# Expert stage of a hybrid encoder block: ScalarE and VectorE in an order written by steps, and two rows in one split

## The chip, the cores and the metric

The kernel runs on one core of a Trainium2 chip. A core has five engines with queues of their own: PE (TensorE, matrix products; PEld in the profile is its weight load), ACT (ScalarE), DVE (VectorE), POOL (GpSimd) and SP (SyncE, which here issues transfers). Each works its instructions off in order; semaphores hold an instruction until what it needs is there. The metric is the device time of one launch in microseconds (us), lower is better.

## The reference

The reference computes one encoder block on x, 1024 tokens of width 2048: attention over a 2D neighbourhood and a two-sided long convolution side by side, an output projection, and a mixture of 16 experts. Only the experts matter here:

```python
affinity = softmax(h @ w_router)              # 1024 x 16
gate, idx = top_k(affinity.T, 128)            # every expert picks its 128 best tokens
xg = h[idx]                                   # 16 x 128 x 2048
a  = xg @ w_gate                              # 2048 -> 1024, per expert
up = xg @ w_up
ye = (silu(a) * up) @ w_down                  # 1024 -> 2048
out[idx] += ye * gate
```

All of it is float32. Each expert has 24 MB of weights, which are read once.

## The kernel before

A float32 product is made of three products in fp32r: an operand is split into hi (a cast to fp32r) and lo (the operand minus hi), and hi x hi, lo x hi and hi x lo are added up in PSUM. `split` (lines 58 to 61) does this with two instructions: ScalarE casts (L60), VectorE subtracts (L61). `mm` (L68) is one matmul.

The block runs in phases: projections, attention and convolution first, then the output projection with the router, then the choice of tokens (`topk`), then the expert stage, in `phase3`. That stage starts at about 2200 us of the span and is the only one that the change touches.

**Tokens.** `gather` fetches an expert's 128 rows by an indirect DMA on POOL into xg (one buffer). `turned` transposes four blocks of 128 x 128 on TensorE (L1202) and splits the result: for xg into xh and xl (16 blocks of k), for the product of gate-up into the two planes of h3 (tile el).

**Weights.** 24 tiles of 1 MB an expert (128 x 2048, tile w) come through a ring of 18 buffers; a load goes out when the buffer's last reader is done. The first 16 hold two rows k of w_gate or w_up (alternating, columns 0 to 1023 of row 2kk, then of row 2kk + 1), the last 8 one row of w_down.

**Steps.** TensorE works in steps of six matmuls of 512 columns on one pair of split tiles wh and wl (128 x 1024, four buffers each, so ScalarE can be four steps ahead). An expert has 32 steps of gate-up (L1141 on) and 16 of down (L1168 on). In the first 24 steps of gate-up a step is one row k of one matrix, all 1024 columns, into two of four PSUM banks. The last four rows come in another order so that half of the columns is finished early: first columns 0 to 511 of all four rows, gate and up, then columns 512 to 1023. Before the change, one such step is one row k, 512 columns of gate beside 512 of up; its wh is written by two casts of 512 columns out of two tiles w, and its wl by two subtractions. After the fourth of these eight steps, `act(0)` takes Silu of the gate sums on ScalarE (L1135) and multiplies with the up sums on VectorE (L1136); after the eighth, `act(1)` does the other half. `turn(0)` and `turn(1)` transpose the products into h3. `down` ends with four copies of PSUM sums, scaled by the gate, into el (L1179), and an indirect DMA on POOL (L1180) that adds the rows to the output. During down, the next expert's xg is transposed.

**Order.** Only TensorE's instructions stand in the order of the program; for ScalarE, VectorE and POOL, a scheduler decides where they stand (L1190):

```python
with tc.manual_schedule(engines={mybir.EngineType.PE}):
```

Of the kernel before, what the change touches and what calls it, by code (L numbers as in the profile page):

```python
# [8 lines left out]
R = mybir.dt.float32r  # L9
I32 = mybir.dt.int32  # L10
U32 = mybir.dt.uint32
AF = mybir.ActivationFunctionType
# [5 lines left out]
P = 128  # L18
D = 2048
S = 1024  # L20
KD = D // P
# [3 lines left out]
NE = 16  # L25
FF = 1024
# [11 lines left out]
class Block:  # L38
# [1029 lines left out]
    def phase3(self, ctx):  # L1068
        tc, nc, a = self.tc, self.nc, self.a
        self.topk()  # L1070
        pa = ctx.enter_context(tc.tile_pool(name="pa", bufs=1, space=PSUM, reuse_waits="tile"))
        pt_ = ctx.enter_context(tc.tile_pool(name="pt3", bufs=2, space=PSUM, reuse_waits="tile"))

        ex = ctx.enter_context(tc.tile_pool(name="ex", bufs=1, reuse_waits="tile"))
        self.ring(ctx, "ewb", 2, side="right")
        self.ring(ctx, "ewc", 8)
        el = self.el = ctx.enter_context(tc.tile_pool(name="el", bufs=1, reuse_waits="tile"))
        self.ring(ctx, "ewd", 5)
        xh = el.tile([P, KD, P], R, name="xh", bufs=1)
        xl = el.tile([P, KD, P], R, name="xl", bufs=1)  # L1080

        def bank():
            return pa.tile([P, 512], F32, name="pa", bufs=6)

        def gather(e):
            if e == NE:
                return
            xg = ex.tile([P, D + 16], F32, name="xg", bufs=1)
            nc.gpsimd.indirect_dma_start(out=xg, out_offset=None, in_=self.xg[:, :],
                                         in_offset=bass.IndirectOffsetOnAxis(ap=self.idx[:, e:e + 1], axis=0))  # L1090
            return xg

        def load():
            ahead = self.EW + max(min(self.used, KD - self.EX) + self.EX, self.used)
            while self.loaded < min(ahead, NE * self.NW):
                self.load_expert()

        def raw():
            load()
            self.used += 1  # L1100
            return self.eraw.pop(0)

        def parts():
            return (el.tile([P, FF], R, name="wh3", bufs=4), el.tile([P, FF], R, name="wl3", bufs=4))

        def products(out, hi, lo, wh, wl, start, stop):

            parts_ = [(o, slice(i * 512, i * 512 + 512)) for i, o in enumerate(out)]
            for o, sl in parts_:
                self.mm(o, hi, wh[:, sl], start, False)  # L1110
                self.mm(o, lo, wh[:, sl], False, False)
            for o, sl in parts_:
                self.mm(o, hi, wl[:, sl], False, stop)

        def half(w, i):
            wh, wl = parts()
            self.split(wh, wl, w[:, i * FF:i * FF + FF])
            return wh, wl

        def gate_up(e):  # L1120


            xg = self.xg3
            rs = ex.tile([P, 16], F32, name="rs", bufs=1)
            nc.scalar.copy(rs[:, 0:1], xg[:, D:D + 1])
            ps = {}
            for n in range(2):
                for j in range(2):
                    ps[j, n] = bank()
            y = el.tile([P, 2 * FF], F32, name="el0", bufs=1)  # L1130
            h3 = el.tile([P, 2, FF // P, P], R, name="el1", bufs=1)

            def act(n):
                s = y[:, n * 512:n * 512 + 512]
                nc.scalar.activation(s, ps[0, n], AF.Silu, scale=rs[:, 0:1])  # L1135
                nc.vector.scalar_tensor_tensor(s, ps[1, n], rs[:, 0:1], s, op0=ALU.mult, op1=ALU.mult)  # L1136

            def turn(n):
                self.turned(pt_, h3[:, 0], h3[:, 1], y, n)

            for kk in range(KD // 2 - 2):  # L1141
                if kk == 2:
                    self.xg3 = gather(e + 1)
                for j in range(2):
                    w = raw() if kk or e else None
                    for i in range(2):
                        wh, wl = half(w, i) if w is not None else ready.pop(0)
                        k = 2 * kk + i
                        products([ps[j, 0], ps[j, 1]], xh[:, k], xl[:, k], wh, wl, k == 0, False)

            w = [raw() for j in range(4)]
            for n in range(2):
                for i in range(4):
                    wh, wl = parts()
                    for j in range(2):
                        sl = slice(j * 512, j * 512 + 512)
                        c = i % 2 * FF + n * 512
                        self.split(wh[:, sl], wl[:, sl], w[i // 2 * 2 + j][:, c:c + 512])
                    if n == 1 and i == 2:
                        turn(0)  # L1160
                    k = KD - 4 + i
                    products([ps[0, n], ps[1, n]], xh[:, k], xl[:, k], wh, wl, False, i == 3)
                act(n)
            return h3, y, lambda: turn(1)

        def down(e, h):
            h3, y, rest = h
            ps = [bank() for n in range(4)]  # L1168
            for k in range(FF // P):
                w = raw()  # L1170
                for c in range(2):
                    wh, wl = half(w, c)
                    products(ps[2 * c:2 * c + 2], h3[:, 0, k], h3[:, 1, k], wh, wl, k == 0, k == FF // P - 1)
                if k == 1:
                    rest()
                elif 3 <= k < 7 and self.xg3 is not None:
                    self.turned(pt_, xh, xl, self.xg3, k - 3, 2)
            for n in range(4):
                nc.scalar.activation(y[:, n * 512:n * 512 + 512], ps[n], AF.Copy, scale=self.gate[:, e:e + 1])  # L1179
            nc.gpsimd.indirect_dma_start(out=a["out"],  # L1180
                                         out_offset=bass.IndirectOffsetOnAxis(ap=self.idx[:, e:e + 1], axis=0),
                                         in_=y, in_offset=None, compute_op=ALU.add)

        self.xg3 = gather(0)
        ready = []
        with tc.issue_after(self.first_cast.ins), tc.issue_after(self.first_sub.ins):
            for j in range(2):
                w = raw()
                ready += [half(w, i) for i in range(2)]
        with tc.manual_schedule(engines={mybir.EngineType.PE}):  # L1190
            for kg in range(4):
                self.turned(pt_ if kg < 2 else pa, xh, xl, self.xg3, kg, 2)
            for e in range(NE):
                down(e, gate_up(e))
# [96 lines left out]
```

## Time and profile before

| | us |
|---|---|
| median of 3 runs | 3332.66 |
| the runs | 3318.23, 3332.66, 3337.95 |
| profiled execution, its own time | 3327.52 |
| its span in the profile | 3325.7 |
| PE busy | 3210.5 (97%) |
| DVE busy | 2331.7 (70%) |
| ACT busy | 1844.1 (55%) |

The profile shows one execution. A timeline row has the start in us from the span's beginning, the length, engine, line and operation, the tiles (out<-in), and how many alike it merges; in brackets stands how long the engine had been idle before it, and whose event ended that. Lengths of matmuls are modelled and overlap; how fast TensorE goes is read from the distance of starts.

### The profile page before, as it was taken

The numbers are of one execution on the slowest core, as the hardware profiler recorded it, in microseconds if no ns is written. First come the engines' busy times: TensorE is split into PE (matmuls) and PEld (weight loads), VectorE is DVE, ScalarE is ACT, GpSimd is POOL, SyncE is SP. The second block draws the span as 40 slices with busy tenths as digits, with TensorE's granted clock in tenths as the row PEclk, the third lists the DMA queues.
The fourth block names the chain that finished last, engine by engine and source line by source line (L and its number), as shares of the span: only waits on it lengthen the run. The fifth ranks groups of instructions, "written<-read, shape, count | busy, mean of one in ns | idle before, by whom it ended". The sixth has DMA issues, their size and how long they took to land.

```text
span 3325.7 us, 47509 instructions
## 1 busy us (share of the span) xinstructions
PE 3210.5 (97%) x17232; PEld 2794.1 (84%) x17232; DVE 2331.7 (70%) x3624; ACT 1844.1 (55%) x2957; POOL 77.3 (2%) x200
## 2 busy tenths in 40 slices
PE   8999999999999999999999999949999999999998
PEld 8899999987888888889977787748888888887886
DVE  5676776764566666667654333289999999898997
ACT  5455655543333333334454232348888888888886
POOL 0000000000000000000000000000000000000000
PEclk9999999999999999999999999979999999999999
DMA  7645555556566556665556464289999999999993
GB/s 248 200 164 163 164 179 186 173 160 209 192 198 197 190 185 196 190 202 167 178 202 230 152 231 152 102 351 360 403 390 403 403 397 394 379 394 399 395 398 116
DMA packets 286571, 830.71 MB, mean 250 GB/s; under 512 B 26340, under 2 KB 105359, under 8 KB 229760
## 3 DMA queue, kind: packets, MB, share of 16 engines
q1 hardware_dynamic: 280544, 791.12, 65.4%
q0 software_dynamic: 5648, 36.49, 4.3%
q8 instruction: 136, 2.23, 0.3%
q14 instruction: 99, 0.81, 0.1%
q10 hardware_dynamic: 144, 0.07, 0.0%
HBM read 751.71 MB, written 75.60 MB: 249 GB/s over the span
## 4 chain that ended last, share of the span: by engine, by line
PE 86%; DMA 7%; issue 2%; ACT 2%; DVE 2%; SPq 0%; POOLq 0%; POOL 0%; ACTq 0%; DVEq 0%
PE pj L68 30%; PE pa L68 29%; PE o L68 7%; PE c L68 5%; PE f L68 4%; PE a L68 3%; PE ct L79 2%; DMA w<-in_w_out_dram 2%; PE tp L1202 1%; ACT wh L60 1%; PE a L79 1%; PE ft L79 1%; DVE wl L61 1%; PE l L68 1%; DMA x<-in_x_dram 1%
## 5 line engine op out<-in xcount | busy, mean ns | idle before, releaser
L60 ACT CAST wh<-w 128x1024 fp32r<-128x1024 f32 (+3 forms) x1368 | 1067.1, 795 | 685.5 <-PE pj L68 374.2
L61 DVE TENSOR_TENSOR wl<-w,wh 128x1024 fp32r<-128x1024 f32 (+3 forms) x1368 | 1210.6, 904 | 336.2 <-ACT wh L60 280.7
L68 PE MATMUL pa<-wh,xh 128*128 128x512 f32 x1024 | 401.5, 392 | 8.4 <-ACT wh L60 8.4
L68 PE MATMUL pa<-wh,xl 128*128 128x512 f32 x1024 | 398.9, 390 | 0.0
L68 PE MATMUL o<-wh,m 128*128 128x512 f32 x1008 | 332.7, 402 | 1.8 <-ACT wh L60 1.7
L68 PE MATMUL pj<-wh,hh 128*128 128x384 f32 x896 | 315.3, 352 | 2.9 <-ACT wh L60 2.9
L68 PE MATMUL pa<-wl,xh 128*128 128x512 f32 x1024 | 317.6, 390 | 0.0
L68 PE MATMUL pj<-hh,wh 128*128 128x512 f32 x768 | 315.2, 411 | 0.0
L68 PE MATMUL pj<-hl,wh 128*128 128x512 f32 x768 | 304.9, 397 | 4.9 <-DMA hl<-lo_d 4.8
L68 PE MATMUL pj<-wl,hh 128*128 128x384 f32 x896 | 304.5, 340 | 0.0
L68 PE MATMUL pj<-wh,hl 128*128 128x384 f32 x896 | 304.1, 339 | 0.0
L68 PE MATMUL pj<-hh,wl 128*128 128x512 f32 x768 | 303.0, 395 | 0.0
L68 PE MATMUL pa<-wh,el 128*128 128x512 f32 x1024 | 281.9, 397 | 0.0
L68 PEld LDWEIGHTS pa<-wh,xh 128*128 128x128 f32 x1024 | 192.4, 188 | 51.3 <-ACT wh L60 12.7
L68 PEld LDWEIGHTS pa<-wl,xh 128*128 128x128 f32 x1024 | 192.2, 188 | 43.7 <-DVE wl L61 3.7
L68 PEld LDWEIGHTS o<-wh,m 128*128 128x128 f32 x1008 | 192.7, 192 | 41.8 <-ACT wh L60 3.4
L68 PEld LDWEIGHTS pa<-wh,xl 128*128 128x128 f32 x1024 | 192.4, 188 | 39.1
L68 PEld LDWEIGHTS pa<-wh,el 128*128 128x128 f32 x1024 | 187.3, 189 | 35.3
L68 PE MATMUL o<-wl,m 128*128 128x512 f32 x504 | 201.0, 400 | 0.3 <-DVE wl L61 0.3
L68 PEld LDWEIGHTS pj<-wh,hh 128*128 128x128 f32 x896 | 169.5, 189 | 8.7 <-ACT wh L60 3.2
L68 PEld LDWEIGHTS pj<-hh,wl 128*128 128x128 f32 x768 | 144.7, 188 | 34.7
L68 PEld LDWEIGHTS pj<-wl,hh 128*128 128x128 f32 x896 | 169.6, 189 | 2.6 <-DVE wl L61 1.1
(307 smaller groups left out, 5275.5 us busy)
## 6 DMA issues: line engine op xcount, KB each, us to landing
hl<-lo_d SPq DMA_DIRECT2D x608, 256.0 KB, 3.0
w<-in_w_down_dram SPq DMA_DIRECT2D x128, 1024.0 KB, 11.4
w<-in_w_up_dram SPq DMA_DIRECT2D x127, 1024.0 KB, 9.1
w<-in_w_gate_dram SPq DMA_DIRECT2D x127, 1024.0 KB, 9.1
w<-in_w_at_dram SPq DMA_DIRECT2D x120, 384.0 KB, 3.4
w<-in_w_out_dram SPq DMA_DIRECT2D x64, 512.0 KB, 4.2
w<-in_w_hy_dram SPq DMA_DIRECT2D x96, 256.0 KB, 3.5
Hd<-H SPq DMA_DIRECT2D x32, 513.0 KB, 4.2
```

What stands on the lines that cost most here:

```text
L60: nc.scalar.copy(hi, src)
L61: nc.vector.tensor_tensor(lo, src, hi.bitcast(F32), op=ALU.subtract)
L68: self.nc.tensor.matmul(out, w, x, start=start, stop=stop)
L79: self.nc.tensor.transpose(pt[:, i * P:(i + 1) * P], b, self.ident)
L1202: self.nc.tensor.transpose(pt[:, i * P:(i + 1) * P], src[:, c:c + (P - 1) * step + 1:step], self.ident)
```

## The change

The casts, subtractions, Silu and copies of the expert stage now stand on ScalarE and VectorE in the order in which the program is written, as TensorE's do: `manual_schedule` lists all three engines. The program is written in steps: `pieces` yields the parts of w that the steps need, in TensorE's order, `prepare` splits the next one, and each call of `products` ends with a `prepare`, so a split is always four steps ahead of its use. What has to stand between the matmuls of a step and the next split (`act`, and `out`, the scaled copies of two down sums) is handed in as `then`. `out(0)` now stands after the last step of sums 0 and 1, one step ahead of `out(1)`.

In the last eight steps of gate-up, a step is now one tile w: two rows k of one matrix, 512 columns. Its split reads both rows through a view of 2 x 512 in one cast and one subtraction, and its six matmuls go into one PSUM bank.

```diff
-        def half(w, i):
-            wh, wl = parts()
-            self.split(wh, wl, w[:, i * FF:i * FF + FF])
-            return wh, wl
+        def pieces():
+            for e in range(NE):
+                for i in range(KD - 4):
+                    w = raw()
+                    yield w[:, :FF]
+                    yield w[:, FF:]
+                w = [raw() for i in range(4)]
+                for n in range(2):
+                    for i in range(4):
+                        yield w[i].rearrange("p (i f) -> p i f", i=2)[:, :, n * 512:n * 512 + 512]
+                for k in range(FF // P):
+                    w = raw()
+                    yield w[:, :FF]
+                    yield w[:, FF:]
+
+        todo, ready = pieces(), []
+
+        def prepare():
+            w = next(todo, None)
+            if w is not None:
+                wh, wl = el.tile([P, FF], R, name="wh3", bufs=4), el.tile([P, FF], R, name="wl3", bufs=4)
+                if len(w.shape) == 3:
+                    self.split(*(x.rearrange("p (i f) -> p i f", i=2) for x in (wh, wl)), w)
+                else:
+                    self.split(wh, wl, w)
+                ready.append((wh, wl))
+
+        def products(parts, then=None):
+            wh, wl = ready.pop(0)
+            for m, (o, hi, lo, start, stop) in enumerate(parts):
+                self.mm(o, hi, wh[:, m * 512:m * 512 + 512], start, False)
+                self.mm(o, lo, wh[:, m * 512:m * 512 + 512], False, False)
+            for m, (o, hi, lo, start, stop) in enumerate(parts):
+                self.mm(o, hi, wl[:, m * 512:m * 512 + 512], False, stop)
+            if then is not None:
+                then()
+            prepare()
...
-            w = [raw() for j in range(4)]
             for n in range(2):
                 for i in range(4):
-                    wh, wl = parts()
-                    for j in range(2):
-                        sl = slice(j * 512, j * 512 + 512)
-                        c = i % 2 * FF + n * 512
-                        self.split(wh[:, sl], wl[:, sl], w[i // 2 * 2 + j][:, c:c + 512])
                     if n == 1 and i == 2:
                         turn(0)
-                    k = KD - 4 + i
-                    products([ps[0, n], ps[1, n]], xh[:, k], xl[:, k], wh, wl, False, i == 3)
-                act(n)
+                    kk, j = KD // 2 - 2 + i // 2, i % 2
+                    products([(ps[j, n], xh[:, k], xl[:, k], False, k == KD - 1) for k in (2 * kk, 2 * kk + 1)],
+                             (lambda: act(n)) if i == 3 else None)
...
+            def out(c):
+                for n in (2 * c, 2 * c + 1):
+                    nc.scalar.activation(y[:, n * 512:n * 512 + 512], ps[n], AF.Copy, scale=self.gate[:, e:e + 1])
+
             for k in range(FF // P):
...
-            for n in range(4):
-                nc.scalar.activation(y[:, n * 512:n * 512 + 512], ps[n], AF.Copy, scale=self.gate[:, e:e + 1])
...
-        with tc.manual_schedule(engines={mybir.EngineType.PE}):
+        with tc.manual_schedule(engines={mybir.EngineType.PE, mybir.EngineType.Activation, mybir.EngineType.DVE}):
```

Three places show what moves. The first is ScalarE in the last eight steps of the seventh expert's gate-up. A number behind wh names the buffer of one step, one behind w the tile that is read. Before (steps 1 to 6; 26209 is step 1, 26271 step 6):

```order
L60 CAST wh_26209<-w_25784 128x512
L60 CAST wh_26221<-w_25784 128x512
L60 CAST wh_26209<-w_25813 128x512
L60 CAST wh_26221<-w_25813 128x512
L60 CAST wh_26233<-w_25842 128x512
L60 CAST wh_26245<-w_25842 128x512
L60 CAST wh_26259<-w_25784 128x512
L60 CAST wh_26259<-w_25813 128x512
L60 CAST wh_26271<-w_25784 128x512
L60 CAST wh_26271<-w_25813 128x512
L60 CAST wh_26233<-w_25871 128x512
L60 CAST wh_26245<-w_25871 128x512
```

With the change (steps 1 to 7, then `act(0)`, then step 8):

```order
L60 CAST wh_26095<-w_25663 128x1024
L60 CAST wh_26105<-w_25692 128x1024
L60 CAST wh_26115<-w_25714 128x1024
L60 CAST wh_26125<-w_25743 128x1024
L60 CAST wh_26135<-w_25663 128x1024
L60 CAST wh_26145<-w_25692 128x1024
L60 CAST wh_26155<-w_25714 128x1024
L1159 ACTIVATE el_25857<-pa,rs 128x512
L60 CAST wh_26167<-w_25743 128x1024
```

Before, the second halves of steps 3 and 4 (26233, 26245) stand behind both halves of steps 5 and 6; now each step has one cast, in step order. Experts 7 to 16 are ordered alike before; in experts 1 to 6 the halves stand in step order:

```order
L60 CAST wh_25600<-w_25175 128x512
L60 CAST wh_25600<-w_25204 128x512
L60 CAST wh_25612<-w_25175 128x512
L60 CAST wh_25612<-w_25204 128x512
L60 CAST wh_25624<-w_25233 128x512
L60 CAST wh_25624<-w_25262 128x512
L60 CAST wh_25636<-w_25233 128x512
L60 CAST wh_25636<-w_25262 128x512
```

These are steps 1 to 4 of the sixth expert; in the change's listing the same steps have one row each, as above.

The second place is VectorE at the end of the seventh expert's gate-up, from the subtraction ahead of `act(0)`'s product to the low half of h3 (el<-tp). Before:

```order
L61 TENSOR_TENSOR wl_26303<-w_25842,wh_26302 128x512
L1136 SCALAR_TENSOR_TENSOR el_25933<-pa,rs,el_25933 128x512
L61 TENSOR_TENSOR wl_26303<-w_25871,wh_26302 128x512
L61 TENSOR_TENSOR wl_26323<-w_25900,wh_26322 128x1024
L61 TENSOR_TENSOR wl_26333<-w_25900,wh_26332 128x1024
L61 TENSOR_TENSOR el_25934<-tp_26289,el_25934 128x512
```

With the change:

```order
L61 TENSOR_TENSOR wl_26156<-w_25714,wh_26155 128x1024
L1160 SCALAR_TENSOR_TENSOR el_25857<-pa,rs,el_25857 128x512
L61 TENSOR_TENSOR wl_26168<-w_25743,wh_26167 128x1024
L61 TENSOR_TENSOR wl_26180<-w_25772,wh_26179 128x1024
L61 TENSOR_TENSOR wl_26190<-w_25772,wh_26189 128x1024
L61 TENSOR_TENSOR el_25858<-tp_26193,el_25858 128x512
```

The product now stands a half subtraction earlier, and three whole subtractions lie between it and the low half of h3, where two and a half did.

The third place is ScalarE at the end of the seventh expert's down. Before:

```order
L60 CAST xh<-tp_26502 128x512
L60 CAST wh_26568<-w_26113 128x1024
L1179 ACTIVATE el_25933<-pa,gate 128x512 x4
L60 CAST wh_26578<-w_26113 128x1024
L60 CAST wh_26590<-w_26135 128x1024
```

With the change:

```order
L60 CAST xh<-tp_26410 128x512
L1186 ACTIVATE el_25857<-pa,gate 128x512 x2
L60 CAST wh_26427<-w_25999 128x1024
L1186 ACTIVATE el_25857<-pa,gate 128x512 x2
L60 CAST wh_26439<-w_25999 128x1024
L1149 COPY rs<-xg 128x1
L60 CAST wh_26460<-w_26021 128x1024
```

Two of the four copies of down sums moved ahead of a cast, and the small copy into rs, which stood in the middle of down before, moved behind all of them. Through it, POOL's gather of the expert after next now stands behind the scatter of this one; it stood ahead of it.

## Rows read from the trace of the kernel before

**Rows 1.** The page, part 1: busy us, share of the span, instructions.

```profile
PE 3210.5 (97%) x17232; PEld 2794.1 (84%) x17232; DVE 2331.7 (70%) x3624; ACT 1844.1 (55%) x2957; POOL 77.3 (2%) x200
```

**Rows 2.** Stretches: length, busy us by engine, granted clock, DMA share, GB/s.

```profile
2285.00:2355.00 70.00, 70.00 (x321) 58.17 (x321) 64.76 (x67) 58.43 (x71) 3.07 (x2) 1.00 1.01 395
...
2705.00:2775.00 70.00, 69.16 (x315) 56.93 (x314) 63.39 (x65) 57.12 (x70) 3.09 (x2) 1.00 1.01 393
```

**Rows 3.** Timeline of POOL, experts two to four: gathers and a scatter.

```profile
2344.47 1.50 POOL L1089 DMA_INDIRECT xg<-xg,idx  x1 [62.82 <-ACT xh L60]
2348.33 1.57 POOL L1180 DMA_INDIRECT out_dram<-el,idx  x1 [2.35 <-ACT el L1179]
...
2481.03 1.53 POOL L1089 DMA_INDIRECT xg<-xg,idx  x1 [62.63 <-ACT xh L60]
```

**Rows 4.** All waits of PE, 2208 to 3326: us in total, times, longest.

```profile
PE pa L68 <- ACT wh L60: 8.4, 10, 0.8
PE tp L1202 <- DVE el L1136: 0.9, 1, 0.9
```

**Rows 5.** Timeline of PE around the seventh expert's wait.

```profile
2655.04 0.39 PE L68 MATMUL pa<-wh,xl 128*128 128x512 f32 x1
2656.27 0.50 PE L68 MATMUL pa<-wh,xh 128*128 128x512 f32 x1 [0.84 <-ACT wh L60]
2656.60 0.39 PE L68 MATMUL pa<-wh,xl 128*128 128x512 f32 x1
```

**Rows 6.** Timeline of PE: the last of the ten waits.

```profile
3283.07 0.50 PE L68 MATMUL pa<-wh,xh 128*128 128x512 f32 x1 [0.84 <-ACT wh L60]
```

**Rows 7.** Timeline of ACT, seventh expert, casts of the last eight steps.

```profile
2647.76 0.62 ACT L60 CAST wh<-w 128x512 fp32r<-128x512 f32 x1 [0.30 <-PE pa L68]
2649.12 2.19 ACT L60 CAST wh<-w 128x512 fp32r<-128x512 f32 x4 [0.74 <-PE pa L68]
...
2654.56 2.18 ACT L60 CAST wh<-w 128x512 fp32r<-128x512 f32 x4 [0.22 <-PE pa L68]
```

**Rows 8.** Groups by form from 2080 on: busy us, mean ns | idle before.

```profile
L61 DVE TENSOR_TENSOR wl<-w,wh 128x1024 fp32r<-128x1024 f32 x647 | 777.6, 1224 | 87.8 <-ACT wh L60 43.0
L60 ACT CAST wh<-w 128x1024 fp32r<-128x1024 f32 x647 | 674.7, 1055 | 160.2 <-PE pa L68 147.6 <-DMA w<-in_w_out_dram 8.1 <-PE o L68 0.3
...
L61 DVE TENSOR_TENSOR wl<-w,wh 128x512 fp32r<-128x512 f32 x248 | 160.2, 688 | 18.7 <-ACT wh L60 13.5
...
L60 ACT CAST wh<-w 128x512 fp32r<-128x512 f32 x248 | 142.1, 618 | 42.8 <-PE pa L68 30.8 <-DVE wl L61 12.0
...
L1136 DVE SCALAR_TENSOR_TENSOR el<-pa,rs,el 128x512 f32<-128x512 f32 x32 | 23.9, 745 | 1.2 <-ACT el L1135 1.2
```

**Rows 9.** Groups by form, whole span: reads that are not plain.

```profile
L244 ACT COPY raw<-pj 128x512 f32<-128x512 f32 x32 | 18.8, 586 | 35.8 <-PE pj L68 35.6
...
L668 DVE TENSOR_TENSOR Z<-Z,c 128x512 f32<-128x512 f32 x16 | 11.0, 688 | 17.2 <-PE c L68 17.2
```

**Rows 10.** Timeline of PE, output projection: one bank, three matmuls between starts.

```profile
2150.12 0.61 PE L68 MATMUL o<-wh,m 128*128 128x512 f32 x2
2150.57 0.39 PE L68 MATMUL o<-wl,m 128*128 128x512 f32 x1
2150.80 0.61 PE L68 MATMUL o<-wh,m 128*128 128x512 f32 x2
```

**Rows 11.** Timelines of DVE and PE where the sixth expert's down starts.

```profile
2593.97 0.69 DVE L61 TENSOR_TENSOR el<-tp,el 128x512 fp32r<-128x512 f32 x1
...
2595.18 1.07 PE L68 MATMUL pa<-wh,el 128*128 128x512 f32 x4
```

**Rows 12.** Timeline of ACT: the last expert's copies of down sums.

```profile
3312.46 2.62 ACT L1179 ACTIVATE el<-pa,gate 128x512 f32<-128x512 f32 x4 [3.25 <-PE pa L68]
```

**Rows 13.** DMA issues in 2285:2354, then 2490:2558: count, KB, us to landing.

```profile
w<-in_w_down_dram SPq DMA_DIRECT2D x8, 1024.0 KB, 11.9
...
w<-in_w_down_dram SPq DMA_DIRECT2D x8, 1024.0 KB, 11.4
```

More of the change, by code (lines that the diff above doesn't have):

```diff
@@ L1101, in raw @@
             return self.eraw.pop(0)
[L1103 to L1113, printed above, removed]
-        def half(w, i):
-            wh, wl = parts()
-            self.split(wh, wl, w[:, i * FF:i * FF + FF])
-            return wh, wl
+        def pieces():
[32 more added lines that the diff above has]
+            prepare()
         def gate_up(e):
@@ L1144, in gate_up @@
                 for j in range(2):
[L1145 to L1149, printed above, removed]
-            w = [raw() for j in range(4)]
+                    for k in (2 * kk, 2 * kk + 1):
+                        products([(ps[j, n], xh[:, k], xl[:, k], k == 0, False) for n in range(2)])
             for n in range(2):
                 for i in range(4):
-                    wh, wl = parts()
-                    for j in range(2):
-                        sl = slice(j * 512, j * 512 + 512)
-                        c = i % 2 * FF + n * 512
-                        self.split(wh[:, sl], wl[:, sl], w[i // 2 * 2 + j][:, c:c + 512])
                     if n == 1 and i == 2:
                         turn(0)
-                    k = KD - 4 + i
-                    products([ps[0, n], ps[1, n]], xh[:, k], xl[:, k], wh, wl, False, i == 3)
-                act(n)
+                    kk, j = KD // 2 - 2 + i // 2, i % 2
+                    products([(ps[j, n], xh[:, k], xl[:, k], False, k == KD - 1) for k in (2 * kk, 2 * kk + 1)],
+                             (lambda: act(n)) if i == 3 else None)
             return h3, y, lambda: turn(1)
@@ L1168, in down @@
             ps = [bank() for n in range(4)]
+            def out(c):
+                for n in (2 * c, 2 * c + 1):
+                    nc.scalar.activation(y[:, n * 512:n * 512 + 512], ps[n], AF.Copy, scale=self.gate[:, e:e + 1])
             for k in range(FF // P):
-                w = raw()
                 for c in range(2):
-                    wh, wl = half(w, c)
-                    products(ps[2 * c:2 * c + 2], h3[:, 0, k], h3[:, 1, k], wh, wl, k == 0, k == FF // P - 1)
+                    products([(ps[2 * c + n], h3[:, 0, k], h3[:, 1, k], k == 0, k == FF // P - 1) for n in range(2)],
+                             (lambda: out(c)) if k == FF // P - 1 else None)
                 if k == 1:
@@ L1184, in phase3 @@
         self.xg3 = gather(0)
-        ready = []
         with tc.issue_after(self.first_cast.ins), tc.issue_after(self.first_sub.ins):
-            for j in range(2):
-                w = raw()
-                ready += [half(w, i) for i in range(2)]
-        with tc.manual_schedule(engines={mybir.EngineType.PE}):
+            for i in range(4):
+                prepare()
+        with tc.manual_schedule(engines={mybir.EngineType.PE, mybir.EngineType.Activation, mybir.EngineType.DVE}):
             for kg in range(4):
```

## The prediction

> **What bounds the kernel now.** I read the page first: TensorE is busy for 97% of the span [rows 1]. A busy share is an average, so next come the stretches of the expert stage, the last third of the span and the only part the change touches. There TensorE is busy 70.00 us of 70 early in the stage and 69.16 later, at full granted clock (1.00, the 2.4 GHz level), while ScalarE has 57 to 58 us of work and VectorE 63 to 65 [rows 2]. So TensorE is the bound, and only time in which it stands still can be won.
>
> Then the pace. Two gathers that stand two experts apart start at 2344.47 and 2481.03 [rows 3]: 136.56 / 2 = **68.28 us an expert**. That is 48 steps and 24 transposes. The casts show the step: ScalarE is let go by TensorE every 1.36 us (2647.76, 2649.12) [rows 7]. 48 x 1.36 = 65.28, which leaves 3.00 us for six groups of four transposes, 0.50 each. An expert in which TensorE never waits takes 68.28 us.
>
> Then the waits of TensorE in the stage. There are only two kinds [rows 4]: ten of 0.84 us on ScalarE's cast into wh, 8.4 us in all, and one of 0.94 us on VectorE's product into el, ahead of a transpose. The wait of 0.84 understates its price. TensorE's matmuls start at 2655.04 and then at 2656.27 [rows 5], 1.23 us apart where 0.23 is usual, and it restarts slowly. The first and the last of the ten stand at 2656.27 and 3283.07, nine experts apart [rows 5, 6]: 626.80 / 9 = 69.64 us an expert. Each of these experts costs 69.64 - 68.28 = **1.36 us** more than an undisturbed one.
>
> Why do they wait? The order listing of the seventh expert tells. In its last eight steps, ScalarE casts the first halves of steps 3 and 4 (wh_26233 and wh_26245), then both halves of steps 5 and 6, and only then the second halves of steps 3 and 4. The casts of steps 5 and 6 write buffers that TensorE frees only when it has done steps 1 and 2. So the second half of step 3, which TensorE needs right after step 2, stands in ScalarE's queue behind a cast that waits for the end of step 2. The timeline agrees: a block of four casts starts at 2654.56 and lasts 2.18 us [rows 7], so they start 0.52 apart; the third of them is the second half of step 3. It ends at 2654.56 + 2 x 0.52 + 0.62 = 2656.22, and TensorE goes on at 2656.27. Experts one to six have the halves in step order, the last ten the knotted one; that is the count of the waits.
>
> **The change, part by part.**
>
> *Order of ScalarE and VectorE by steps.* In the new order the cast of a step always stands behind the cast of the step before it, and four steps ahead of its use. The knot is gone in all ten experts: 10 x 1.36 = **13.6 us**. In the first expert the Silu stood behind all sixteen half casts; now it stands ahead of the last step's cast, so the product into el comes earlier and the 0.94 us before the transpose goes: **0.9 us**. What is late next? After that TensorE waits for nothing, and its own 68.28 us is the floor.
>
> *One two-row split for two half splits.* Sixteen 512-wide casts and sixteen subtractions an expert become eight of each, 1024 wide. Per step, if a two-row read costs what a plain one does, ScalarE saves 2 x 618 - 1055 = 181 ns and VectorE 2 x 688 - 1224 = 152 ns [rows 8]. Both engines have spare time [rows 2], TensorE covers it: 0 us. No expert-stage row shows a read in two runs. From above I bound it by twice the plain 1024 (2.45 us on VectorE), from below by the plain 1.224. The nearest rows are a ScalarE copy that reads two runs out of two banks (586 ns for 512, against 618 for a plain 512 cast) and a VectorE addition that reads every second element (688 ns, as a plain one) [rows 9]. I take the plain value.
>
> *Matmuls of a step into one bank.* In the last eight steps all six matmuls now add into one accumulator. In the output projection they do so already: starts of 2150.12 and 2150.80 with three matmuls between [rows 10], 0.227 each, and 1.36 / 6 is 0.227 too. From below a gain is excluded by that equality; from above I see no row that is slower. 0 us.
>
> *The Silu, the products and the transposes of h3.* On VectorE three subtractions stand between the product into el and the low half of h3, which the second matmul of the down stage reads. In the sixth expert (undisturbed) that low half was done at 2593.97 + 0.69 = 2594.66, and the matmul came at 2595.18 + 0.23 = 2595.41 [rows 11]: 0.75 us to spare. For the new order I count from the end of the fourth of the last eight steps, call it 0. The cast ahead of the Silu starts at latest at -1.36 and takes 1.05, its subtraction 1.22: VectorE is free at 0.92. Then 0.745 for the product, 3 x 1.224 and 0.69 [rows 8, 11]: 6.02. The matmul comes at 4 x 1.36 + 0.50 + 0.23 = 6.17. **0.15 us to spare**, with no overlap of neighbours counted, though the rows do overlap (four casts of 618 in 2.18 us, not 2.47 [rows 7]). 0 us, but this is the tightest place.
>
> *The copies of the down sums.* ScalarE now takes sums 0 and 1 one step earlier, ahead of a cast, and waits there for TensorE; behind it stand the casts of the next expert's second and third gate-up steps. From the end of the last step but one of down: two copies at 2.62 / 4 = 0.66 [rows 12] end at 1.31, a cast at 2.37, two more copies at 3.68, the next cast at 4.73, its subtraction at 5.96. That step starts at 4 x 1.36 = 5.44 and reads its low half four matmuls later, at 6.35: 0.39 us to spare, 0 us. After the last expert, the first two copies already run before TensorE ends (start 3312.46 [rows 12]), so the tail wins nothing.
>
> *POOL.* The gather of the expert after next now stands behind the scatter (before, it started 3.9 us ahead of it: 2344.47 against 2348.33 [rows 3]), since the copy into rs that frees its buffer moved behind the down copies. It is needed after 32 steps of gate-up and 8 of down, 40 x 1.36 = 54 us later: 0 us. The loads on SP keep their order.
>
> Sum: 13.6 + 0.9 = 14.5 us. The profiled execution took 3327.52 us (span 3325.7 and 1.8 around it): 3327.5 - 14.5 = **3313 us**. It lies 5 us under the median of the three runs shown, 3332.66.
>
> **Rivals.**
>
> *The weight stream becomes the bound* (7%). At 68.28 us an expert the DMAs must bring 395 GB/s x 68.28 us = 27.0 MB. If the 393 GB/s of the disturbed experts [rows 2] were all they can do, with their 69.64 x 393 = 27.4 MB, an expert would stay at 69.6 us and the time at about 3327 us. For it: the DMA share is 1.01 all through [rows 2]. Against it: experts two to six ran at 68.28 with 395 GB/s, and the loads of w_down took 11.9 us to land at the beginning of that stretch and 11.4 near its end [rows 13]: the queue didn't grow. The Trainium skill, Perfetto Trace Analysis, section Roofline, has a figure that speaks against the change: it counts throughput against 358 GB/s, a core's share when both cores of a pair draw. By that figure 27.0 MB would take 75 us an expert, and nothing on ScalarE could help. The trace disagrees, with 395 GB/s measured; the same section lets a core that draws alone reach about 435 GB/s, and with that the trace agrees.
>
> *The low half of h3 comes late* (8%). If the count above is short by up to one subtraction (1.22 us), every expert stands still that long: 16 x 1.22 = 19.5 us against 14.5 won, 3332 us. Against it: the 0.75 us of [rows 11], with a VectorE that then had more work queued.
>
> *The two-row split is slow, the one that ends on the other side* (4%). At 2.45 us a subtraction, eight steps in a row are 8 x (2.45 - 1.36) = 8.7 us late. The four-step lead takes up 3 x 1.36 + 0.91 - 1.05 - 1.22 = 2.7 us of it. 6.0 us an expert, 96 in all: 3409 us. It decides from 1.36 + 2.7 / 8 = 1.70 us a subtraction on. Against it: [rows 9].
>
> That the change doesn't do what it says is excluded by the listing.
>
> **Numbers.** The forecast itself has 78%; the three rivals 19%; 3% stay for what I don't see. The forecast's own range comes from the scatter of the runs shown: 3318.2 - 14.5 = 3304 to 3338.0 - 14.5 = 3323. Taking in the two rivals without a gain up to about 3330, I give **3302 to 3330**. A measurement of this kernel can't tell less than about 1% (33 us) from no change. A gain of 14.5 us, 0.4%, lies within it; more can't come from a TensorE floor, so over 1% faster only by scatter: 4%. Slower by over 1% needs the third rival or the unseen: 6%. Within 1%: 90%.
>
> **What would show it.** The waits of TensorE on wh and on el in the stage should be gone (0 to 1 us in all), all experts 68.3 us apart, TensorE busy 70.0 of 70 to the end at 396 to 400 GB/s. The two-row casts should last about 1.05 us, their subtractions about 1.22. The low half of h3 should end before the second matmul of down; a wait of TensorE on el there would be the second rival. Landing times that climb from 11 us towards 40 would be the first. Durations above 1.7 us on VectorE would be the third. I would be wrong if TensorE's waits went and the experts stayed 69.6 us apart.

## The result and the profile after

The changed kernel took 3311.1 us (median of 13 runs, 3306.02 to 3315.45), the kernel before, on the same chip, 3329.18 us (13 runs, 3315.23 to 3337.95). The ratio is 0.9949, with a 95% interval of 0.9935 to 0.9962: 17 us less, between 13 and 22, which is 0.5%. The forecast was 3313 us, 0.4% less than before.

The page of the profiled execution (3306.56 us, span 3304.8), part 1, answers to [rows 1]:

```profile
PE 3201.5 (97%) x17232; PEld 2793.3 (85%) x17232; DVE 2322.4 (70%) x3496; ACT 1832.3 (55%) x2829; POOL 84.9 (3%) x200
```

The shares are those of before, give or take one point; 128 instructions fewer stand on VectorE and on ScalarE each. The stretches of the expert stage, as in [rows 2] (length, busy us of PE, PEld, DVE, ACT, POOL, granted clock, DMA share, GB/s), tell more:

```profile
2285.00:2355.00 70.00, 70.00 (x322) 58.15 (x321) 64.11 (x58) 57.61 (x63) 3.61 (x2) 1.00 1.01 401
2705.00:2775.00 70.00, 70.00 (x321) 58.16 (x321) 64.02 (x58) 57.59 (x63) 3.60 (x2) 1.00 1.01 400
```

TensorE is now busy 70.00 us of 70 late in the stage too, where it was 69.16. The DMAs bring 400 GB/s there, 393 before. The waits of TensorE from 2195 us on (engine, tile and line, whom it waited for: us in total, times, longest), and the row of the second:

```profile
PE tp L1216 <- DMA xg<-xg,idx: 7.6, 1, 7.6
PE pa L68 <- DVE el L61: 0.2, 1, 0.2
...
2246.85 0.98 PE L68 MATMUL pa<-wh,el 128*128 128x512 f32 x3 [0.24 <-DVE el L61]
```

The first is the gather of the first expert's rows, which stands in both kernels ahead of the stage. The ten waits on wh and the one on el of [rows 4] are gone; one new wait of 0.24 us, on the low half of h3, stands in the first expert. The timeline of POOL answers to [rows 3], and goes further into the stage:

```profile
2193.02 1.10 POOL L1089 DMA_INDIRECT xg<-xg,idx  x1 [407.93 <-DMA w<-in_w_down_dram]
...
2343.48 2.04 POOL L1089 DMA_INDIRECT xg<-xg,idx  x1 [0.30 <-ACT wh L60]
...
2480.04 2.04 POOL L1089 DMA_INDIRECT xg<-xg,idx  x1 [0.30 <-ACT wh L60]
...
3026.34 2.04 POOL L1089 DMA_INDIRECT xg<-xg,idx  x1 [0.30 <-ACT wh L60]
...
3162.92 2.04 POOL L1089 DMA_INDIRECT xg<-xg,idx  x1 [0.30 <-ACT wh L60]
```

Two experts take 136.56 us early (2480.04 - 2343.48) and 136.58 late: 68.28 and 68.29 an expert. The late ones took 69.64 before. ScalarE's timeline in the seventh expert, at the end of its gate-up, answers to [rows 7]:

```profile
2647.61 1.06 ACT L60 CAST wh<-w 128x1024 fp32r<-128x1024 f32 x1 [0.30 <-PE pa L68]
2648.97 1.06 ACT L60 CAST wh<-w 128x1024 fp32r<-128x1024 f32 x1 [0.30 <-PE pa L68]
2649.93 0.68 ACT L1159 ACTIVATE el<-pa,rs 128x512 f32<-128x512 f32 x1
2650.51 2.24 ACT L60 CAST wh<-w 128x1024 fp32r<-128x1024 f32 x2
```

The casts wait 0.30 us each for the buffer that TensorE lets go, step after step, and the Silu starts at once when its turn comes. The two-row casts shown, 1.06 us each, are as long as the plain ones. The groups by form from 2080 on (busy us, mean ns | idle before) say the same of all 1024-wide splits, a sixth of which now read two rows:

```profile
L61 DVE TENSOR_TENSOR wl<-w,wh 128x1024 fp32r<-128x1024 f32 x771 | 927.0, 1223 | 101.3 <-ACT wh L60 43.9
L60 ACT CAST wh<-w 128x1024 fp32r<-128x1024 f32 x771 | 805.2, 1055 | 191.7 <-PE pa L68 177.0 <-DMA w<-in_w_out_dram 7.4 <-DVE wl L61 4.9
```

They are 1223 and 1055 ns, as in [rows 8]. Where does the time come from, in the two profiled executions? The stage lies between the first gather and the last expert's copies. The first gather of before, and the last copies of the change:

```profile
2199.29 1.10 POOL L1089 DMA_INDIRECT xg<-xg,idx  x1 [413.40 <-DMA w<-in_w_down_dram]
...
3291.93 2.62 ACT L1186 ACTIVATE el<-pa,gate 128x512 f32<-128x512 f32 x4 [3.25 <-PE pa L68]
```

With [rows 12] and the gather of 2193.02 above, the stage took 3312.46 - 2199.29 = 1113.2 us before and takes 3291.93 - 2193.02 = 1098.9 now: 14.3 us. It also starts 6.3 us earlier, though the change touches nothing ahead of it. That part arose in the output projection. The columns are those of [rows 2], before first:

```profile
1840.00:2110.00 270.00, 262.18 (x1223) 215.72 (x1221) 86.91 (x127) 80.26 (x123) 0.00 (x0) 0.96 0.51 172
...
1840.00:2110.00 270.00, 261.66 (x1254) 215.84 (x1253) 89.04 (x130) 82.40 (x125) 0.00 (x0) 0.99 0.52 176
```

TensorE's granted clock, here a mean over its two levels of 1.2 and 2.4 GHz, was 0.96 in the one execution and 0.99 in the other, and TensorE did 1223 matmuls in the one and 1254 in the other; up to 1840 us it had done 10782 and 10783. The 31 matmuls at 0.227 us [rows 10] are 7 us. In the profiles of the six experiments below, with the same work ahead, the first gather starts between 2188.04 and 2196.64, so I count this part as scatter between executions and not as a gain of the change. What sets the clock in a single execution, no run here shows.

### The profile page after: what moved, and what is told of

It reads as the page before. It is cut to its first block, busy times and chain, and to the rows that moved or that the text cites. A ratio compares the mean times of both kernels' runs of the same rounds, so it can differ in the third digit from the quotient of the medians.

```text
span 3304.8 us, 47172 instructions
## 1 busy us (share of the span) xinstructions
PE 3201.5 (97%) x17232; PEld 2793.3 (85%) x17232; DVE 2322.4 (70%) x3496; ACT 1832.3 (55%) x2829; POOL 84.9 (3%) x200
## 4 chain that ended last, share of the span: by engine, by line
PE 87%; DMA 6%; DVE 2%; issue 2%; ACT 2%; SPq 0%; POOLq 0%; POOL 0%; ACTq 0%; DVEq 0%
PE pj L68 30%; PE pa L68 29%; PE o L68 7%; PE c L68 6%; PE f L68 4%; PE a L68 3%; PE ct L79 2%; DMA w<-in_w_out_dram 2%; PE tp L1216 1%; PE a L79 1%; PE ft L79 1%; DVE wl L61 1%; PE l L68 1%; DMA x<-in_x_dram 1%; DMA w<-in_w_up_dram 1%
## 5 line engine op out<-in xcount | busy, mean ns | idle before, releaser
L61 DVE TENSOR_TENSOR wl<-w,wh 128x1024 fp32r<-128x1024 f32 (+2 forms) x1244 | 1200.6, 979 | 327.0 <-ACT wh L60 261.3
L60 ACT CAST wh<-w 128x1024 fp32r<-128x1024 f32 (+2 forms) x1244 | 1057.0, 857 | 669.6 <-PE pj L68 385.2
## 6 DMA issues: line engine op xcount, KB each, us to landing
w<-in_w_down_dram SPq DMA_DIRECT2D x128, 1024.0 KB, 11.8
```

What stands on the lines that cost most here:

```text
L60: nc.scalar.copy(hi, src)
L61: nc.vector.tensor_tensor(lo, src, hi.bitcast(F32), op=ALU.subtract)
```

## The experiments

My theory: ScalarE works its queue off in order, so an instruction in it that waits for TensorE holds up every cast behind it; where TensorE needs one of these next, it stands still. Before the change, the knotted halves (second halves of steps 3 and 4 queued behind casts that wait, as the prediction describes) did that in ten experts. The rivals: it is the smaller amount of work on ScalarE and VectorE; it is some other place in the written order.

**Order without the merge.** The written order of the change, with two half splits:

```diff
                 if len(w.shape) == 3:
-                    self.split(*(x.rearrange("p (i f) -> p i f", i=2) for x in (wh, wl)), w)
+                    for i in range(2):
+                        sl = slice(i * 512, i * 512 + 512)
+                        self.split(wh[:, sl], wl[:, sl], w[:, i])
```

> The written order on ScalarE and VectorE as in the change, but the two-row splits of the last eight steps of gate-up are again two casts and two subtractions of 512 columns, one behind the other. Theory (the knot: second halves of steps 3 and 4 stood behind casts that wait for TensorE): no knot here, all experts 68.3 us apart, TensorE waits under 1 us in the stage, time as with the change, 3311 us, 0.5% under before. Rival (less work on ScalarE and VectorE made the gain): the work is that of before, so TensorE still waits on wh once an expert from the seventh on, 69.6 us apart, time as before, 3329 us.

Measured: 3314.9 us, ratio to before 0.9957 (0.9940 to 0.9974), not to be told from the change's. Its timeline of POOL, late in the stage:

```profile
3029.02 2.03 POOL L1089 DMA_INDIRECT xg<-xg,idx  x1 [0.30 <-ACT wh L60]
3097.31 2.03 POOL L1089 DMA_INDIRECT xg<-xg,idx  x1 [0.30 <-ACT wh L60]
```

That is 68.29 us an expert, with the work of before on both engines. The order alone brings the gain; the rival on the amount of work is out. What the merge adds in the profile lies in the first expert, which takes 70.2 us here (first matmuls of experts one and two at 2203.51 and 2273.74) and 69.0 with the change (2202.06 and 2271.07).

**The merge without the order.** One line: only TensorE's order is written.

```diff
-        with tc.manual_schedule(engines={mybir.EngineType.PE, mybir.EngineType.Activation, mybir.EngineType.DVE}):
+        with tc.manual_schedule(engines={mybir.EngineType.PE}):
```

> The two-row splits of the change, but only TensorE's order is written; ScalarE and VectorE stand where the scheduler puts them (by the listing: every step's cast in step order, the Silu sometimes one cast later, the four copies of down sums in one block, the small copy into rs in the middle of down). Theory (the knot): a step has one cast, there are no halves to knot, so 68.3 us an expert and 3311 us. Rival (the written order as a whole, with its place for Silu and copies, made the gain): 69.6 us an expert from the seventh on, about 3329 us.

Measured: 3353.0 us, ratio 1.0075 (1.0058 to 1.0093): slower than before. Both expectations, 3311 and 3329 us, missed. Without halves there is no knot of halves, but TensorE waits more than before (its waits from 2195 us on):

```profile
PE pa L68 <- ACT wh L60: 17.1, 10, 1.7
...
PE tp L1216 <- DVE el L1160: 6.1, 10, 0.9
PE pa L68 <- DVE el L61: 3.2, 9, 0.4
```

What I wrote of its listing holds for the first six experts only. From the seventh on, the scheduler puts the first Silu four casts earlier than the change has it, behind the cast of the third of the last eight steps and ahead of the fourth's:

```
L60 CAST wh_26115<-w_25714 128x1024
L1159 ACTIVATE el_25857<-pa,rs 128x512
L60 CAST wh_26125<-w_25743 128x1024
```

The Silu needs the gate sums that TensorE finishes in step 3. ScalarE's timeline there:

```profile
2645.65 1.06 ACT L60 CAST wh<-w 128x1024 fp32r<-128x1024 f32 x1 [0.30 <-PE pa L68]
2651.54 0.69 ACT L1159 ACTIVATE el<-pa,rs 128x512 f32<-128x512 f32 x1 [4.84 <-PE pa L68]
2652.13 6.72 ACT L60 CAST wh<-w 128x1024 fp32r<-128x1024 f32 x7
```

And TensorE's:

```profile
2653.21 0.50 PE L68 MATMUL pa<-wh,xh 128*128 128x512 f32 x1 [1.71 <-ACT wh L60]
...
2658.54 0.66 PE L1216 MATMUL tp<-ident,el 128*128 128x128 f32 x4 [0.59 <-DVE el L1160]
...
2662.55 0.96 PE L68 MATMUL pa<-wh,el 128*128 128x512 f32 x3 [0.36 <-DVE el L61]
```

ScalarE stands still for 4.84 us with four casts behind it whose buffers come free meanwhile. Then it casts as fast as it can, seven in a row, but step 4 is late by 1.71 us, and the rest of the delay shows on VectorE's results. Its gathers at 2757.04 and 2829.18 are 72.14 us apart, 3.86 over TensorE's own 68.28; ten such experts make 39 of the 42 us that this kernel takes more than the change. The next run tests whether the knot was one case of a wider cause: a wait ahead of a cast that is needed sooner.

**The Silu early, in the written order.** To separate the Silu from what else differs there (copies in one block, the copy into rs earlier), the change with the Silu moved to that place, in experts 2 to 16:

```diff
-            prepare()
+            for i in range(ahead):
+                prepare()
...
-                             (lambda: act(n)) if i == 3 else None)
+                             (lambda: act(n)) if i == 3 else (lambda: silu(0)) if e and i == 2 and n == 0 else None,
+                             1 if not e or n else (0, 0, 4, 1)[i])
```

The last step of the loop ahead of these has `ahead` 0 as well.

> As the change with its written order and its two-row splits, but in experts 2 to 16 the first Silu stands on ScalarE where the scheduler put it in the merge-only kernel from the seventh expert on: behind the cast of the third of the last eight steps and ahead of the casts of steps 4 to 7 (in the change it stands behind the cast of step 7). VectorE's order stays. Theory (a ScalarE instruction that waits for TensorE, placed ahead of a cast that TensorE needs next, is what costs; it need not be a half split): the Silu waits some 4.8 us for the gate sums of step 3, the casts of steps 4 to 7 start only then, TensorE stands still about 1.7 us on wh at step 4 and shorter on el behind it, 72.1 us an expert as in the merge-only kernel: 15 x 3.85 = 58 us more, 3311 + 58 = 3369 us. Rival (the block of four copies or the early copy into rs made the merge-only kernel slow): 3311 us.

Measured: 3367.5 us, ratio 1.0125 (1.0099 to 1.0151). TensorE's waits:

```profile
PE pa L68 <- ACT wh L60: 25.7, 15, 1.7
PE tp L1224 <- DVE el L1166: 7.0, 12, 0.6
PE pa L68 <- DVE el L61: 4.8, 13, 0.4
```

Two of its gathers, two experts apart:

```profile
2342.52 2.03 POOL L1089 DMA_INDIRECT xg<-xg,idx  x1 [0.30 <-ACT wh L60]
...
2486.78 2.04 POOL L1089 DMA_INDIRECT xg<-xg,idx  x1 [0.30 <-ACT wh L60]
```

There are fifteen waits of 1.71 us, and two experts take 144.26 us by the gathers: 72.13 an expert, where the kernel without the written order had 72.14. The Silu's place alone makes it; 3369 us was expected.

**The knot in all experts.** Written order, half splits, and the halves in the order of before's experts 7 to 16, now in all sixteen:

```diff
...
+                half(0)
+                if p < 4:
+                    self.held.append(lambda: half(1))
+                else:
+                    half(1)
+                if p == 1 or p == 5:
+                    for i in range(2):
+                        self.held.pop(0)()
...
```

(p counts the last eight steps from 0; half(i) is the split of one half.)

> Written order with half splits, and the halves of the last eight steps set by hand as experts 7 to 16 of before have them (steps 1 2 1 2 3 4 5 5 6 6 3 4 7 7 8 8), now in all sixteen experts. Theory (the knot): each expert costs 1.36 us more, sixteen waits of 0.84 us on wh, 69.64 us apart, 3311 + 16 x 1.36 = 3333 us, which is 0.1% above before. Rival (the knot is harmless, something else in the scheduler's order made the waits): 68.3 us apart, 3311 us.

Measured: 3339.8 us, ratio 1.0034 (1.0020 to 1.0048). TensorE's waits:

```profile
PE pa L68 <- ACT wh L60: 13.5, 16, 0.8
```

Two of its gathers, two experts apart:

```profile
2348.60 2.04 POOL L1089 DMA_INDIRECT xg<-xg,idx  x1 [0.30 <-ACT wh L60]
...
2488.07 2.04 POOL L1089 DMA_INDIRECT xg<-xg,idx  x1 [0.30 <-ACT wh L60]
```

There are sixteen waits on wh, of 0.84 us each, where ten made 8.4 us in [rows 4]. Two experts take 2488.07 - 2348.60 = 139.47 us, 69.74 each. Against the kernel with order and half splits but no knot the time is 3339.8 - 3314.9 = 25 us longer, 1.56 an expert; 1.36 was expected (3333 us), and the profile has 69.74 - 68.28 = 1.46. The knot is the cause, and it costs what the ten experts said, or slightly more. Both engines had the knotted order here; no run set it on ScalarE alone, but it is ScalarE's cast that the waits name.

**Three steps ahead instead of four.**

```diff
...
-            for i in range(4):
+            for i in range(3):
                 prepare()
...
```

(In the first expert the split stands ahead of Silu and copies, since tiles y and h3 lie in buffers that the splits must have read by then.)

> As the change, but every split stands three steps ahead of its use in the order instead of four (the first expert keeps the Silu and the copies behind the split, since its buffers ask for that). The buffers stay four, so in quiet stretches nothing changes. Theory (the lead is what carries ScalarE over the copies of down sums, which wait for TensorE: with four steps 0.39 us were to spare, with three the casts behind them come one step, 1.36 us, later): TensorE waits on wh at the first steps of experts 2 to 16, about 0.4 us twice, with the restart some 0.7 to 1.0 us a seam, 15 seams, 11 to 16 us: 3322 to 3327 us. Rival (four buffers alone set how far ScalarE is ahead): 3311 us.

Measured: 3320.4 us, ratio 0.9974 (0.9961 to 0.9988), 9 us over the change and 2 under the range that I expected. Experts 3 to 16 take 69.01 us, 0.73 more. ScalarE's timeline at a seam, where one expert ends and the next begins:

```profile
2479.22 1.27 ACT L1189 ACTIVATE el<-pa,gate 128x512 f32<-128x512 f32 x2 [0.57 <-PE pa L68]
2480.37 1.05 ACT L60 CAST wh<-w 128x1024 fp32r<-128x1024 f32 x1
2481.31 1.28 ACT L1189 ACTIVATE el<-pa,gate 128x512 f32<-128x512 f32 x2
2482.47 1.06 ACT L60 CAST wh<-w 128x1024 fp32r<-128x1024 f32 x1
```

And TensorE's at the third step of the new expert's gate-up:

```profile
2482.89 0.63 PE L68 MATMUL pa<-wl,xh 128*128 128x512 f32 x2
2483.58 0.50 PE L68 MATMUL pa<-wh,xh 128*128 128x512 f32 x1
2483.91 0.39 PE L68 MATMUL pa<-wh,xl 128*128 128x512 f32 x1
...
2484.38 0.39 PE L68 MATMUL pa<-wh,xl 128*128 128x512 f32 x1
2484.84 0.73 PE L68 MATMUL pa<-wl,xh 128*128 128x512 f32 x2
```

The second cast ends at 2483.53 and the step that needs it starts at 2483.58; its low half comes late too (2484.84 instead of 2484.61). The place is as expected, and so are two short waits, though they are shorter than the 0.4 us expected and both in this one step, one on the high part and one on the low. The view of waits shows none of this: the modelled lengths of the matmuls before cover gaps that short. They are seen in the distance of starts (0.46 us where 0.23 is usual: from 2484.38 to 2484.84, and from the second matmul of the row of 2482.89, at about 2483.12, to 2483.58).

So the buffers alone don't set how far ScalarE is ahead. Order decides: with three steps of lead, a cast that is needed sooner stands behind the copies that wait.

**The copies in one block.** The change with the four copies of down sums behind the last step, as before:

```diff
-                             (lambda: out(c)) if k == FF // P - 1 else None)
+                             (lambda: (out(0), out(1))) if k == FF // P - 1 and c else None)
```

> As the change, but the four copies of down sums stand in one block behind the last step of down, as before the change, with the cast of the next expert's second step ahead of them. Theory: these copies have slack in either place, TensorE doesn't wait, 68.3 us an expert, 3311 us. Rival (their earlier place is part of the gain): TensorE waits at the seam of experts, some 0.5 us or more each, 3319 us or above.

Measured: 3307.6 us, ratio 0.9938 (0.9919 to 0.9957), not to be told from the change's 0.9949. The gathers at 2344.98 and 2481.70 give 68.36 us an expert, 0.08 over the change, or 1.2 us in all in the profile. (The cast that stands ahead of the block is that of the next expert's third step.) The earlier place of two copies is worth next to nothing.

## Why the prediction was right

*TensorE is the bound, 68.28 us an expert is its floor.* Right: 68.28 and 68.29 early and late, and in no kernel of the study did an expert take less.

*Ten knots at 1.36 us, 13.6 us.* Right in mechanism and size. Order alone undoes them, the knot by hand brings sixteen waits of the same length, and the stage gained 14.3 us in the profile.

*The first expert, 0.9 us.* Too large: the wait of 0.94 us on el went, but one of 0.24 on the low half of h3 came. The first matmuls of experts one and two are now 69.0 us apart (2202.06 and 2271.07), after 69.6 (2208.41 and 2278.02), so 0.6 of 0.9 came.

*The sum, 14.5 us.* 14.3 measured in the stage's profile. The ratio's interval of 13 to 22 us holds it; its middle, 17 us, is above, and no row of the stage accounts for more than 14.3. The interval allows that this is scatter, and the beginnings in the eight profiles, which differ by up to 11 us with the same work, show such scatter; the 3 us between the two stay open. That 3313 lies 2 us from 3311.1 is in part luck: the sum started from one execution of 3327.52, and from the median of 13, 3329.18, it gives 3314.7. The prediction was too cautious where it held that less than 1% can't be told from no change: the interval leaves out 1.

*The two-row split at the plain price, 0 us from the merge.* Right: 1055 and 1223 ns, and the kernel without the merge is as fast within its interval.

*One bank for six matmuls, 0 us.* Right: 68.28 us an expert is unchanged.

*The low half of h3, the tightest place, 0.15 us to spare.* No wait there from the second expert on, as forecast, with more room than the count gave. The timelines of VectorE and TensorE in the sixth expert of the change answer to [rows 11]; VectorE first:

```profile
2584.70 2.36 DVE L61 TENSOR_TENSOR wl<-w,wh 128x1024 fp32r<-128x1024 f32 x2
2586.99 0.68 DVE L61 TENSOR_TENSOR el<-tp,el 128x512 fp32r<-128x512 f32 x1
```

```profile
2588.23 1.07 PE L68 MATMUL pa<-wh,el 128*128 128x512 f32 x4
```

2588.23 + 0.23 - 2587.67 = 0.79 us are to spare, 0.75 before. Counting whole lengths one behind the other was too strict: neighbours on VectorE overlap (two subtractions of 1.22 us each take 2.36 in the first row). The product also started earlier, 0.62 us after the end of the fourth step (2582.91 after 2582.29) instead of 0.92.

*The copies, 0.39 us to spare at the seam.* Right that nothing waits with four steps of lead, and with three a wait came at just this place; but the count was again too strict. The casts behind the copies are those of the next expert's third and fourth steps, not of the second and third as the prediction calls them; its sum goes to the fourth, which is the right one. ScalarE and VectorE there, with the change:

```profile
2750.92 1.06 ACT L60 CAST wh<-w 128x1024 fp32r<-128x1024 f32 x1
...
2752.01 9.17 DVE L61 TENSOR_TENSOR wl<-w,wh 128x1024 fp32r<-128x1024 f32 x8 [0.88 <-ACT wh L60]
```

The first of these subtractions ends about 2752.01 + 1.22 = 2753.23, and the fourth step, which starts at 2753.15, reads its low half at 2754.06: 0.83 us to spare. One step less of lead, 1.36 us, is more than that.

*POOL, 0 us.* Right: the gather stands behind the scatter and nobody waits for it, though it is now listed with 2.04 us where it had 1.53.

*The rivals.* The weight stream didn't become the bound: 400 GB/s at 68.28 us an expert. The w_down loads took 11.8 us to land early (2285 to 2354 us) and 12.6 late in the stage (3040 to 3110):

```profile
w<-in_w_down_dram SPq DMA_DIRECT2D x8, 1024.0 KB, 11.8
...
w<-in_w_down_dram SPq DMA_DIRECT2D x8, 1024.0 KB, 12.6
```

That is no climb towards 40 us. The low half of h3 came late only in the first expert, by 0.24 us, and the two-row splits were no slower.

## What to carry to other kernels

In an engine's queue, look for instructions that wait for the bound engine and ask what stands behind them: what is needed soonest must not be behind a wait that ends later. A scheduler's order can differ between repetitions of the same loop (six good experts, ten bad ones), so read the order of a late repetition, and price its waits by the distance of repetitions, not by the idle time shown. And where a change has two parts, run each alone: here the order is worth all of it within the intervals, and the kernel with the other part alone is 0.75% slower than before, because the scheduler then puts the Silu ahead of casts that are needed sooner.

## What was not expected of the hardware

A wait of 0.84 us costs TensorE 1.36 us in the kernel before and 1.46 with the knot in all experts. The rows behind [rows 5] show where:

```profile
2656.83 0.83 PE L68 MATMUL pa<-wl,xh 128*128 128x512 f32 x2
2657.49 0.39 PE L68 MATMUL pa<-wh,xh 128*128 128x512 f32 x1
```

The starts around the wait stand 1.23 us apart where 0.23 is usual, which is 1.00 and not 0.84, since the modelled end of the matmul before covers a part. The next two are 0.33 apart, 0.10 more. Then two matmuls take 0.66 where 0.45 is usual (2656.83 to 2657.49), 0.21 more, which fits a low half that comes late too. That is 1.31 of the 1.36.

Gaps of about 0.23 us between matmuls are not in the view of waits at all, though at two a seam, with a slower start behind each, they made 0.73 us an expert and 9 us in the kernel with three steps of lead.
